# Another order of the seven half-size products in q, z and layer A's output projection

## The chip, the cores and the metric

The kernel runs on one core of a Trainium2 chip. The metric is the device time of one execution in microseconds, the median of several runs. The kernel before the change takes 2928.23 us (three runs, 2926.15 to 2930.01 us).

A core has five engines that run side by side, each with a queue that it works through in order: TensorE (PE in the profile, with PEld for the loading of its stationary operand), VectorE (DVE), ScalarE (ACT), GpSimd (POOL) and SyncE (SP), which here issues all transfers between the chip's main memory and the on-chip buffer. PE's results land in PSUM, a small memory that DVE and ACT read.

## The reference, cut to what matters

The model has one gated MLP layer (layer A), shared keys and values, and one layer of dilated attention (layer B), on 2048 tokens of width 1024, all in float32:

```python
def gmlp_layer(x, c, ...):                       # layer A
    h = rms_norm(x, norm_g) * (1 + scale) + shift
    u, v, z = jnp.split(h @ w_in, 3, axis=-1)
    ...
    y = u * mixed.reshape(bsz, s, A_WIDTH) * jax.nn.silu(z)
    return x + gate * (y @ w_out)                # dense_o: (2048 x 2048) @ (2048 x 1024)

def dilated_layer(x, c, kv_groups, ...):         # layer B
    h = rms_norm(x, norm_g) * (1 + scale) + shift
    qz = h @ w_in                                # dense_s: three q blocks and z, 1024 x 1024 each
    q = qz[..., :N_Q_HEADS * HEAD_DIM].reshape(bsz, s, N_Q_HEADS, HEAD_DIM)
    z = qz[..., N_Q_HEADS * HEAD_DIM:]
    q = rms_norm(q, q_norm_g) * (HEAD_DIM ** -0.5)
    for g, (window, d) in enumerate(DILATED_GROUPS):
        ...                                      # attention of group g; g = 2 is the widest
    y = o.reshape(bsz, s, B_WIDTH) * jax.nn.silu(z)
    return x + gate * (y @ w_out)
```

## The kernel before, in words

The tokens are worked in four quarters (Q = 0 to 3) of 512 tokens, four tiles of 128 rows each. A quarter goes through layer A (v, then u, then z, then the output projection), the norms of layer B, and `proj_B`: the third k/v block, the second, the q block of group 2, the first k/v block, the q blocks of groups 1 and 0, and z.

Float32 products are made of three matmuls each (`mm3`, line 278): every operand is split into a high and a low part (`split`, line 249: ACT writes the high part, DVE the rest), and high x high, low x high and high x low are added up in PSUM. One matmul takes a 128 x 128 stationary operand and 512 columns. Weights come by SP's transfers and, except for presplit ones, are split after they land (L251 on ACT, L252 on DVE).

**Seven half-size products.** q, z of layer B and, in quarters 1 to 3, layer A's output are multiplied as 2 x 2 blocks with seven products in place of eight. With A the tokens' operand and B the weights, s1 to s4 are sums of A's quadrants and t1 to t4 sums of B's, made ahead of time. The seven are 11·11, 12·21, s1·t1, s2·t2, s3·t3, s4·22 and 22·t4. Four results come out of them: rows 0 and 1 (tiles t = 0, 1) and rows 2 and 3 (t = 2, 3), each for column half n = 0 and n = 1:

- rows 0, 1, n = 0: 11·11 + 12·21
- U2 = 11·11 + s2·t2, a sum that the other three results share; U3 = U2 + s3·t3
- rows 2, 3, n = 1: U3 + s1·t1
- rows 2, 3, n = 0: U3 + 22·t4
- rows 0, 1, n = 1: U2 + s1·t1 + s4·22

`dense_s` (line 545) does this for a q block or z: 16 calls, four a quarter. It has two pairs of PSUM tiles, x and y, one tile for each row tile i; a product is 24 matmuls into one pair, and successive products alternate between the pairs. The flag `first` says whether a product starts its pair afresh or adds to what stands there. The order before is 11, s2, 12, s3, s1, 22·t4, s4·22; shared sums are kept in on-chip "sum tiles" (`sum_tile`, a pool of eight), to which DVE adds each further product out of PSUM (`add`, L575, ten additions of 128 x 512 a call); ACT copies the first one (L580, two a call). `evac` takes a finished result: for q (`q_block`, L1215) ACT squares, DVE and POOL make the row norms, and the tile goes to memory in `qd` by a store that is put off by some products (`stores`, `store_late`, L270); where a q result stands in PSUM itself, ACT copies it to a sum tile first (L1219). For z (`z_block`, L1235) ACT applies Silu (L1239) and the result goes to `zd`; in quarter 3 six of its eight tiles are held until later.

`dense_o` (line 456) does the same for layer A's output, with products of 48 matmuls, in two halves h, from weights that were combined and split before (`wtd`). Here `rows` names the halves in which all matmuls of row tile 0 go ahead of those of row tile 1. Copies are L503, additions L499, and the evacuation `ev` (L1134) adds a kept sum if it is given one (L1137), multiplies by the gate (L1138), adds the residual (L1109) and has ACT square the sum (L1110); after a row's second half, the row's norm is made and the normed row `xn` written (L1125). The hook, given as `(6, ...)`, puts `norm_T2` (L720) of rows 0 and 1 into the sixth product: 16 transposes on PE (L730), and on DVE the affine maps (L734) and low parts (L737). The same for rows 2 and 3 comes inside the k/v block that follows.

**What sets the order.** The program is written in the order of its Python calls, and work of other stages is mixed in as fillers: generators of which `tick` runs some steps after every few matmuls. In quarters 1 to 3 local attention fills layer A. In quarter 3 the attention of group 2 (`wide_attention`, L1170) fills the first k/v block and the q blocks of groups 1 and 0; it first flushes q2's stores, then loads, unit by unit, 128 rows of `qd` (L1319), taken at a stride of 16 rows from all quarters: column half n = 0 for a block's first unit, n = 1 for its second. A scheduler then orders each engine's instructions at compile time, by priority in the program's order and by when operands will be ready; all waits are put in by it. So one engine's order can differ from the written one, but on the chip it is fixed.

Of the kernel before, what the change touches and what calls it, by code (L numbers as in the profile page):

```python
# [34 lines left out]
def trunk(ctx, tc, out, x, c, a_ada_w, a_ada_b, a_norm_g, a_w_in, a_sgu_g, a_w_spatial,  # L35
# [420 lines left out]
    def dense_o(Q, ops, fs, evac, hook, after):  # L456
# [40 lines left out]
        def add(o, p, q):  # L497
            for i in range(2):
                nc.vector.tensor_tensor(o[i][:, 0:512], p[i], q[i][:, 0:512], ALU.add)  # L499

        def copy(pts, t):
            for i in range(2):
                nc.scalar.activation(t[i][:, 0:512], pts[i], AF.Copy)  # L503
            return t

        product(x, "11", "11", True, lambda: weights("21", 0), rows=(1,))
        u = copy(x, [sum_tile(f"ou{Q}{i}") for i in range(2)])
        operand("s4", "12")
        product(x, "12", "21", False, lambda: weights("22", 0), rows=(0, 1))
        for i in range(2):  # L510
            evac(i, 0, x[i], None)
        operand("s2", "11")
        product(y, "s4", "22", True, lambda: weights("t2", 0))
        q = copy(y, [sum_tile(f"oq{Q}{i}") for i in range(2)])
        operand("s1", "21")
# [3 lines left out]
        product(x, "s2", "t2", True, lambda: weights("t1", 0))  # L519
        add(u, x, u)  # L520
        operand("22", "22")
        product(y, "s1", "t1", True, lambda: weights("t3", 0), rows=(1,))
        w = [rp.tile([P, 512], F32, tag="raw", name=f"ow{Q}{i}") for i in range(2)]
        add(w, y, u)
        for i in range(2):
            evac(i, 1, w[i], q[i][:, 0:512])
        product(x, "s3", "t3", True, lambda: weights("t4", 0), hook)
        for i in range(2):
            evac(2 + i, 1, x[i], w[i])
        add(u, x, u)  # L530
        product(y, "22", "t4", True, after, rows=(1,))
        for i in range(2):
            evac(2 + i, 0, y[i], u[i][:, 0:512])
# [11 lines left out]
    def dense_s(ops, b, nm, evac):  # L545
# [24 lines left out]
        def tmp(n):  # L570
            return [sum_tile(f"{nm}{n}{i}") for i in range(2)]

        def add(o, p, q):
            for i in range(2):
                nc.vector.tensor_tensor(o[i][:, 0:512], p[i], q[i][:, 0:512], ALU.add)  # L575

        product(x, "11", "11", True)
        u2 = tmp("u")
        for i in range(2):
            nc.scalar.activation(u2[i][:, 0:512], x[i], AF.Copy)  # L580
        product(y, "s2", "t2", True)
        add(u2, y, u2)
        product(x, "12", "21", False)
        for i in range(2):
            evac(i, x[i], 0)
# [1127 lines left out]
```

## Time and profile before

| | us |
|---|---|
| runs: median (lowest to highest) | 2928.23 (2926.15 to 2930.01) |
| the profiled execution, first to last instruction | 2930.7 |
| PE busy | 2890.4 |
| DVE busy | 2166.7 |
| ACT busy | 1639.0 |
| POOL busy | 758.4 |

The profiled execution's own time is known by its span, 2930.7 us; it lies 2.5 us above the median of the runs. In the profile, a group's row gives line, engine, operation, output<-inputs, shapes and count, then the busy time in us, the mean of one in ns, and the engine's idle time before it with what ended it. In the windows view, each row is a stretch of the span in us from its start, with its length and the busy time of each engine (instructions in brackets), PE's granted clock, the DMA engines' busy share and GB/s. In the timeline view, each row has the start, the time until the last of the merged instructions ended, engine, line, operation, tensors and count, and in brackets idle time before and what released it. Neighbouring matmuls overlap in these rows: one takes about 390 ns but the next starts some 230 ns later (48 of them take 11.04 us). Names such as `pd_o3a` and `pd_o3b` are the PSUM pairs of dense_o in quarter 3, `pd_q31a` those of the q block of group 1 in quarter 3, `st_...` sum tiles.

### The profile page before, as it was taken

The page shows a single profiled execution, that of the slowest core. Times are in us where ns is not written, and L with a number is a line of the kernel's source. Part 1 is how long each engine was busy: PE and PEld are TensorE (multiplying, and loading weights), DVE is VectorE, ACT ScalarE, POOL GpSimd, SP SyncE. Part 2 cuts the span into 40 slices and gives each one's busy share as a digit, 9 for nine tenths or more (in the row PEclk, how much of TensorE's full clock was granted, in tenths as well). Part 3 has the DMA queues.
Part 4 walks back from the last instruction along what each step waited for, and adds up shares of the span by engine and source line. Part 5 has one row for each costly group of instructions (what it writes and reads, how often), then busy time and mean ns, then how long its engine had stood idle before and what let it go on. Part 6 is the DMA issues. An engine that isn't in the chain of part 4 may idle for free.

```text
span 2930.7 us, 45684 instructions
## 1 busy us (share of the span) xinstructions
PE 2890.4 (99%) x14642; PEld 2422.7 (83%) x14642; DVE 2166.7 (74%) x4038; ACT 1639.0 (56%) x3378; POOL 758.4 (26%) x1043
## 2 busy tenths in 40 slices
PE   8999999999999999999999999999999999999999
PEld 5788888888888878888888888888888888888887
DVE  6878666787777886877677776877769776888682
ACT  4323355767676365676555365674646366876441
POOL 1057522330000513501223213501414221122312
PEclk9999999999999999999999999999999999999999
DMA  8899976796889976887435976875337967789653
GB/s 285 272 311 336 308 244 184 257 306 203 282 294 315 334 241 210 265 289 249 158 120 202 344 226 203 296 262 162 105 109 260 322 202 224 256 271 332 216 172 112
DMA packets 393813, 713.54 MB, mean 243 GB/s; under 512 B 41723, under 2 KB 141277, under 8 KB 393573
## 3 DMA queue, kind: packets, MB, share of 16 engines
q1 hardware_dynamic: 393572, 710.63, 72.6%
q8 instruction: 116, 1.90, 0.3%
q14 instruction: 125, 1.02, 0.1%
HBM read 552.53 MB, written 157.95 MB: 242 GB/s over the span
## 4 chain that ended last, share of the span: by engine, by line
PE 40%; DMA 3%; issue 3%; DVE 3%; POOL 1%; ACT 1%; SPq 0%; POOLq 0%; ACTq 0%; DVEq 0%
PE po L1453 3%; PE pd_kv L280 3%; PE pd_z L324 2%; PE pd_z L322 2%; PE pd_z L323 2%; PE pd_o3a L280 1%; PE pd_u L322 1%; PE pd_u L324 1%; PE pd_u L323 1%; PE pd_o2a L280 1%; PE pd_v3b L280 1%; PE pf L1637 1%; PE pf L1638 1%; PE pf L1639 1%; DMA qt<-qd 1%
## 5 line engine op out<-in xcount | busy, mean ns | idle before, releaser
L280 PE MATMUL pd_kv<-w_kv,hkh 128*128 128x512 f32 x672 | 209.5, 393 | 1.4 <-DVE w_kv L252 1.3
L322 PE MATMUL pd_u<-hAh,w_u 128*128 128x512 f32 x512 | 207.5, 405 | 0.0
L322 PE MATMUL pd_z<-hAh,w_z 128*128 128x512 f32 x512 | 204.1, 399 | 0.0
L324 PE MATMUL pd_u<-hAh,w_u 128*128 128x512 f32 x512 | 201.0, 393 | 2.3 <-DVE w_u L252 2.3
L323 PE MATMUL pd_u<-hAl,w_u 128*128 128x512 f32 x512 | 200.2, 391 | 0.0
L324 PE MATMUL pd_z<-hAh,w_z 128*128 128x512 f32 x512 | 200.2, 391 | 0.0
L323 PE MATMUL pd_z<-hAl,w_z 128*128 128x512 f32 x512 | 199.5, 390 | 0.0
L1453 PEld LDWEIGHTS po<-kv,pT 128*128 128x128 f32 x1200 | 147.9, 192 | 13.0 <-ACT pT L1299 3.7
L251 ACT ACTIVATE w_u<-raw_u 128x512 fp32r<-128x512 f32 x128 | 79.2, 630 | 135.4 <-DMA raw_u<-in_a_w_in_dram 56.7
L1453 PE MATMUL po<-kv,pT 128*128 128x128 f32 x1200 | 151.2, 276 | 3.6 <-ACT pT L1299 2.5
L251 ACT ACTIVATE w_z<-raw_z 128x512 fp32r<-128x512 f32 x128 | 79.6, 628 | 133.9 <-PE pd_z L324 60.6
L280 PEld LDWEIGHTS pd_kv<-w_kv,hkh 128*128 128x128 f32 x672 | 125.9, 189 | 28.6 <-DVE w_kv L252 2.6
L1401 POOL TENSOR_TENSOR dg<-pr,ident 128x256 f32<-128x256 f32 x38 | 30.9, 813 | 437.2 <-DVE stat L1448 226.6
L252 DVE TENSOR_TENSOR w_z<-raw_z,w_z 128x512 fp32r<-128x512 f32 x128 | 109.4, 868 | 44.9 <-ACT w_z L251 44.6
L280 PE MATMUL pd_kv<-w_kv,hkl 128*128 128x512 f32 x336 | 131.2, 391 | 0.0
L1393 ACT ACTIVATE pr<-pr,stat,rt 128x256 f32<-128x256 f32 (+1 forms) x192 | 104.2, 544 | 33.2 <-DVE stat L1387 20.0
L1226 POOL TENSOR_SCALAR s_q<-s_q 128x4 f32<-128x4 f32 x96 | 26.6, 277 | 351.3 <-DVE s_q L1225 238.8
L252 DVE TENSOR_TENSOR w_u<-raw_u,w_u 128x512 fp32r<-128x512 f32 x128 | 94.1, 745 | 30.8 <-ACT w_u L251 30.0
L324 PEld LDWEIGHTS pd_u<-hAh,w_u 128*128 128x128 f32 x512 | 96.4, 188 | 24.2 <-DVE w_u L252 3.1
L251 ACT ACTIVATE w_q<-raw_q 128x512 fp32r<-128x512 f32 x144 | 88.8, 627 | 48.3 <-PE pd_kv L280 11.2
L252 DVE TENSOR_TENSOR w_q<-raw_q,w_q 128x512 fp32r<-128x512 f32 x144 | 95.8, 687 | 24.9 <-ACT w_q L251 22.9
L324 PEld LDWEIGHTS pd_z<-hAh,w_z 128*128 128x128 f32 x512 | 96.1, 188 | 20.7
(904 smaller groups left out, 8553.1 us busy)
## 6 DMA issues: line engine op xcount, KB each, us to landing
raw_q<-in_b_w_in_dram SPq DMA_DIRECT2D x144, 256.0 KB, 3.4
w_o<-wtd SPq DMA_DIRECT2D x72, 512.0 KB, 5.2
raw_u<-in_a_w_in_dram SPq DMA_DIRECT2D x128, 256.0 KB, 4.2
raw_z<-in_a_w_in_dram SPq DMA_DIRECT2D x128, 256.0 KB, 3.6
wtd<-cs SPq DMA_DIRECT2D x56, 512.0 KB, 4.1
qt<-qd SPq DMA_DIRECT2D x96, 260.0 KB, 3.6
raw_v<-in_a_w_in_dram SPq DMA_DIRECT2D x96, 256.0 KB, 4.1
od<-ot SPq DMA_DIRECT2D x96, 256.0 KB, 3.0
```

What stands on the lines that cost most here:

```text
L251: nc.scalar.activation(hi, src, AF.Copy)
L252: nc.vector.tensor_tensor(lo, src, hi.bitcast(F32), ALU.subtract)
L280: last_mm[0] = nc.tensor.matmul(pt, a, u[:, w, :], start=f, stop=e, skip_group_check=more)
L322: nc.tensor.matmul(pts[i], wh, hh[:, k, :], start=k == 0, stop=False)
L323: nc.tensor.matmul(pts[i], wh, hl[:, k, :], start=False, stop=False)
L324: nc.tensor.matmul(pts[i], wl, hh[:, k, :], start=False, stop=k == KT - 1)
L1393: nc.scalar.activation(pr[:, i, :], pr[:, i, :], AF.Exp, bias=mneg[:, i:i + 1], scale=u["rt"][:, h:h + 1], accum_out=lsum[:, i:i + 1])
L1401: nc.gpsimd.tensor_tensor(dg, prev, ident.unsqueeze(1).broadcast_to([P, hp, P]), ALU.mult)
L1453: nc.tensor.matmul(po[:, h * P:(h + 1) * P], u["pT"][h // hp][:, h % hp, j, :], u["kv"][:, j, kh, 1, :], start=j == 0, stop=j == nk - 1)
L1637: nc.tensor.matmul(pt, yb[:, 0, k, :], w_[:, 0, :], start=k == 0, stop=False)
L1638: nc.tensor.matmul(pt, yb[:, 0, k, :], w_[:, 1, :], start=False, stop=False)
L1639: nc.tensor.matmul(pt, yb[:, 1, k, :], w_[:, 0, :], start=False, stop=k == KT - 1)
```

## The change

In `dense_o` and `dense_s` the seven products get the order 11, 12·21, s2, s1, then s3 and s4·22 (dense_s) or s4·22 and s3 (dense_o), then 22·t4. The pair that holds 11·11 is copied by ACT, goes on to take s2·t2 (so it holds U2) and is copied again, then takes s3·t3 (U3) and at last 22·t4, so that rows 2, 3 with n = 0 stand in PSUM as a whole. The other pair takes 12·21, and then s1·t1, which ACT copies, and s4·22 on top. Each of the other three results is one PSUM pair plus one copied sum, added by DVE. The additions of `dense_s` fall from ten to six a call and its copies rise from two to six; in `dense_o` the additions fall from twelve to six (those in `ev` included) and the copies rise from four to six. The operand splits of `dense_o` move with their products, and `rows` is set for other products. In `q_block` the copy out of PSUM moves from rows 0, 1 to rows 2, 3 (n = 0), and in `z_block` the tiles that are not held in quarter 3 change likewise, and their stores are issued at once.

```diff
--- before.py
+++ after.py
@@ -494,43 +494,37 @@
             for h in range(2):
                 split(ops[n][:, h, 0], ops[n][:, h, 1], fs[h][src])
 
-        def add(o, p, q):
+        def copy(pts, nm):
+            t = [sum_tile(f"{nm}{Q}{i}")[:, 0:512] for i in range(2)]
             for i in range(2):
-                nc.vector.tensor_tensor(o[i][:, 0:512], p[i], q[i][:, 0:512], ALU.add)
-
-        def copy(pts, t):
-            for i in range(2):
-                nc.scalar.activation(t[i][:, 0:512], pts[i], AF.Copy)
+                nc.scalar.activation(t[i], pts[i], AF.Copy)
             return t
 
         product(x, "11", "11", True, lambda: weights("21", 0), rows=(1,))
-        u = copy(x, [sum_tile(f"ou{Q}{i}") for i in range(2)])
+        p1 = copy(x, "op")
+        operand("s2", "11")
+        product(y, "12", "21", True, lambda: weights("t2", 0), rows=(1,))
+        for i in range(2):
+            evac(i, 0, y[i], p1[i])
+        operand("s1", "21")
+        product(x, "s2", "t2", False, lambda: weights("t1", 0))
+        u2 = copy(x, "ou")
         operand("s4", "12")
-        product(x, "12", "21", False, lambda: weights("22", 0), rows=(0, 1))
-        for i in range(2):
-            evac(i, 0, x[i], None)
-        operand("s2", "11")
-        product(y, "s4", "22", True, lambda: weights("t2", 0))
-        q = copy(y, [sum_tile(f"oq{Q}{i}") for i in range(2)])
-        operand("s1", "21")
+        product(y, "s1", "t1", True, lambda: weights("22", 0), rows=(1,))
+        p5 = copy(y, "oq")
         for f in fs:
             nc.vector.tensor_tensor(f["11"], f["22"], f["11"], ALU.subtract)
         operand("s3", "11")
-        product(x, "s2", "t2", True, lambda: weights("t1", 0))
-        add(u, x, u)
+        product(y, "s4", "22", False, lambda: weights("t3", 0), rows=(0, 1))
+        for i in range(2):
+            evac(i, 1, y[i], u2[i])
         operand("22", "22")
-        product(y, "s1", "t1", True, lambda: weights("t3", 0), rows=(1,))
-        w = [rp.tile([P, 512], F32, tag="raw", name=f"ow{Q}{i}") for i in range(2)]
-        add(w, y, u)
+        product(x, "s3", "t3", False, lambda: weights("t4", 0), hook, rows=(1,))
         for i in range(2):
-            evac(i, 1, w[i], q[i][:, 0:512])
-        product(x, "s3", "t3", True, lambda: weights("t4", 0), hook)
+            evac(2 + i, 1, x[i], p5[i])
+        product(x, "22", "t4", False, after, rows=(0, 1))
         for i in range(2):
-            evac(2 + i, 1, x[i], w[i])
-        add(u, x, u)
-        product(y, "22", "t4", True, after, rows=(1,))
-        for i in range(2):
-            evac(2 + i, 0, y[i], u[i][:, 0:512])
+            evac(2 + i, 0, x[i], None)
         return nxt.pop()
 
     def load_wo(n, q):
@@ -567,38 +561,32 @@
                 with tc.issue_after(last_ld[0].ins):
                     job()
 
-        def tmp(n):
-            return [sum_tile(f"{nm}{n}{i}") for i in range(2)]
-
-        def add(o, p, q):
+        def copy(pts, n):
+            t = [sum_tile(f"{nm}{n}{i}") for i in range(2)]
             for i in range(2):
-                nc.vector.tensor_tensor(o[i][:, 0:512], p[i], q[i][:, 0:512], ALU.add)
+                nc.scalar.activation(t[i][:, 0:512], pts[i], AF.Copy)
+            return t
+
+        def add(o, p, r, n):
+            for i in range(2):
+                nc.vector.tensor_tensor(o[i][:, 0:512], p[i], o[i][:, 0:512], ALU.add)
+                evac(i + r, o[i], n)
 
         product(x, "11", "11", True)
-        u2 = tmp("u")
+        p1 = copy(x, "u")
+        product(y, "12", "21", True)
+        add(p1, y, 0, 0)
+        product(x, "s2", "t2", False)
+        u2 = copy(x, "v")
+        product(y, "s1", "t1", True)
+        p5 = copy(y, "w")
+        product(x, "s3", "t3", False)
+        add(p5, x, 2, 1)
+        product(y, "s4", "22", False)
+        add(u2, y, 0, 1)
+        product(x, "22", "t4", False)
         for i in range(2):
-            nc.scalar.activation(u2[i][:, 0:512], x[i], AF.Copy)
-        product(y, "s2", "t2", True)
-        add(u2, y, u2)
-        product(x, "12", "21", False)
-        for i in range(2):
-            evac(i, x[i], 0)
-        product(y, "s3", "t3", True)
-        u3 = tmp("v")
-        add(u3, y, u2)
-        product(x, "s1", "t1", True)
-        add(u3, x, u3)
-        for i in range(2):
-            evac(i + 2, u3[i], 1)
-        product(y, "22", "t4", False)
-        c21 = tmp("w")
-        add(c21, y, u2)
-        for i in range(2):
-            evac(i + 2, c21[i], 0)
-        product(x, "s4", "22", False)
-        add(u2, x, u2)
-        for i in range(2):
-            evac(i, u2[i], 1)
+            evac(i + 2, x[i], 0)
 
     def dense_s2(ops, bs, nm, evac, late):
 
@@ -1214,7 +1202,7 @@
 
         def q_block(g):
             def ev(t, src, n):
-                if t < 2 and n == 0:
+                if t >= 2 and n == 0:
                     c_ = sum_tile(f"qc{g}{Q}{t}")
                     nc.scalar.activation(c_[:, 0:512], src, AF.Copy)
                     src = c_
@@ -1234,12 +1222,12 @@
 
         def z_block(_):
             def ev(t, src, n):
-                held = Q == NQ - 1 and (t, n) not in ((0, 0), (1, 0))
+                held = Q == NQ - 1 and (t, n) not in ((2, 0), (3, 0))
                 zt = src[:, 0:512] if held else evt(f"zb{n}{Q}_{t}")
                 nc.scalar.activation(zt, src[:, 0:512], AF.Silu)
                 put = lambda: nc.sync.dma_start(zd[rows(t), n * 512:(n + 1) * 512], zt)
-                if Q == NQ - 1:
-                    stores.append([-100 if held else 3, put])
+                if held:
+                    stores.append([-100, put])
                 else:
                     put()
             dense_s(hb, 3, f"z{Q}b", ev)
```

## The prediction

> **What bounds the kernel now.** I read the page's busy shares first, then the busy time by windows cut at the stages that the change touches, then who waited for whom on PE, then the order of time around two joints.
>
> ```profile
> span 2930.7 us, 45684 instructions
> ...
> PE 2890.4 (99%) x14642; PEld 2422.7 (83%) x14642; DVE 2166.7 (74%) x4038; ACT 1639.0 (56%) x3378; POOL 758.4 (26%) x1043
> ```
>
> PE (TensorE) is busy for 2890.4 of 2930.7 us; DVE (VectorE) and ACT (ScalarE) have slack over the whole span. The span is 2.5 us above the median of the runs, 2928.23; differences are worked out in the span and applied to the median. A change of under 0.2% (5.9 us) is about what a measurement of this kernel can't tell from none.
>
> ```profile
> core 0: us, PE busy (x) PEld busy (x) DVE busy (x) ACT busy (x) POOL busy (x), PEclk, DMA share, GB/s
> 520.00:638.00 118.00, 118.00 (x537) 97.63 (x536) 91.44 (x148) 79.82 (x144) 50.58 (x79) 1.00 0.83 278
> 930.00:1090.00 160.00, 156.63 (x825) 131.18 (x823) 134.40 (x289) 85.06 (x190) 44.30 (x60) 1.00 0.83 292
> 1579.00:1732.00 153.00, 151.13 (x786) 126.91 (x785) 126.95 (x260) 74.59 (x158) 41.16 (x59) 1.00 0.86 298
> 1791.00:1909.00 118.00, 118.00 (x538) 97.59 (x537) 91.93 (x147) 79.11 (x143) 53.99 (x79) 1.00 0.82 272
> 2226.00:2376.00 150.00, 147.99 (x767) 124.70 (x766) 120.79 (x249) 76.33 (x159) 38.28 (x54) 1.00 0.83 286
> 2414.00:2450.00 36.00, 32.69 (x166) 26.92 (x165) 17.80 (x44) 16.59 (x42) 7.63 (x18) 0.95 0.62 195
> 2450.00:2614.00 164.00, 159.69 (x1069) 142.86 (x1069) 132.82 (x336) 135.23 (x382) 26.21 (x55) 1.00 0.79 253
> 2614.00:2656.00 42.00, 41.21 (x185) 33.21 (x184) 28.49 (x53) 25.01 (x48) 9.00 (x15) 1.00 0.98 359
> ```
>
> The rows from 520 and 1791 hold two q blocks and z of quarters 0 and 2: PE has no idle time at all there. The three rows of 150 to 160 us hold layer A's output (dense_o) and the first k/v block of quarters 1 to 3: 3.37, 1.87 and 2.01 us idle. The last three are in quarter 3: the k/v block in which the wide attention starts (3.31 idle), the two q blocks with attention between their products (4.31), and z (0.79). Idle time within the change's reach is thus 15.7 us, 0.5% of the span. No engine's total says more than that.
>
> **The change, part by part.** Removed and added work has these prices:
>
> ```profile
> L499 DVE TENSOR_TENSOR st_ou<-pd_o2a,st_ou 128x512 f32<-128x512 f32 x4 | 2.6, 682 | 0.0
> ...
> L575 DVE TENSOR_TENSOR st_q11v<-pd_q11a,st_q11u 128x512 f32<-128x512 f32 x2 | 1.4, 688 | 1.8 <-PE pd_q11a L280 1.8
> ...
> L580 ACT ACTIVATE st_q31u<-pd_q31b 128x512 f32<-128x512 f32 x2 | 1.1, 584 | 0.0
> ```
>
> Each of the 16 dense_s calls goes from 10 DVE additions to 6 and from 2 copies to 6; each of the 3 dense_o calls from 12 additions to 6 and from 4 copies to 6. That is 64 + 18 = 82 additions less, 82 x 0.685 = 56 us of DVE, and 64 + 6 = 70 copies more, 70 x 0.584 = 41 us of ACT. The matmuls, their weights' loads and the stores stay the same in number.
>
> dense_s in quarters 0 to 2 and q2 of quarter 3: nothing. PE is saturated, and successive products still alternate between the two PSUM pairs, so each read has a whole product's time to finish, as now. If that cover failed, a product would wait for one 0.58 or 0.69 us read at most; 0 is taken. A q call fills all eight sum tiles before and after. The copies after products 3 and 4 now take tiles that the previous call's stores must have left; were one late, ACT would stand, with the weights' splits queued behind the copy, and PE after them. Today the q evacuation's copy after product 3 takes its tile at that same place in windows without idle time, so this too is 0.
>
> dense_o: two joints become tight, since a product now adds to the pair that the product just before it filled. From product 5 on (y, after s1·t1) the wait is for an ACT copy. That joint exists today after product 1, with the products' rows sorted as here:
>
> ```profile
> 1595.27 0.60 ACT L503 ACTIVATE st_ou<-pd_o2a 128x512 f32<-128x512 f32 x1 [0.48 <-PE pd_o2a L280]
> ...
> 1596.51 2.91 PE L280 MATMUL pd_o2a<-w_o,yo 128*128 128x512 f32 x12
> ```
>
> The copy ends at 1595.87 and PE shows no idle time: 0 for this one. The other is from product 6 (x, s3·t3) to 7 (x, 22·t4): PE must wait until DVE has read x in the evacuation, and the hook puts norm_T2's DVE work right there. Today product 7 goes to y and nobody waits:
>
> ```profile
> 2298.13 0.69 DVE L499 TENSOR_TENSOR ow<-pd_o3b,st_ou 128x512 f32<-128x512 f32 x1 [6.00 <-PE pd_o3b L280]
> 2299.92 1.12 DVE L1459 SCALAR_TENSOR_TENSOR ot<-st_o,stat,po 128x128 f32<-128x128 f32 x4 [1.09 <-PE po L1453]
> ...
> 2314.95 0.99 DVE L734 TENSOR_SCALAR h_b_0k<-pt_b,affk,affk 128x256 f32<-128x256 f32 x2 [2.09 <-PE pt_b L730]
> ...
> 2320.63 1.28 DVE L1137 TENSOR_TENSOR xo<-pd_o3a,ow 128x512 f32<-128x512 f32 x2
> ...
> 2325.05 1.28 DVE L499 TENSOR_TENSOR st_ou<-pd_o3a,st_ou 128x512 f32<-128x512 f32 x2
> ...
> 2329.26 0.68 DVE L252 TENSOR_TENSOR w_kv<-raw_kv,w_kv 128x512 fp32r<-128x512 f32 x1
> ```
> ```profile
> 2317.44 11.04 PE L280 MATMUL pd_o3b<-w_o3t,yo 128*128 128x512 f32 x48
> ...
> 2329.99 0.50 PE L280 MATMUL pd_kv<-w_kv,hkh 128*128 128x512 f32 x1 [1.06 <-DVE w_kv L252]
> ```
>
> Product 7 starts at 2317.44, and x is read from 2320.63 on. Product 6 gets sorted rows, so x0 is complete 12 matmuls before x1, and six of them come before the hook. I take x0's read to run before the hook's DVE work, in the 2.09 us for which DVE stood idle ahead of 2314.95: the first two rows show that order today, an addition of product 5's first half ahead of an attention step (L1459) that the program writes earlier. Then only x1's read is late. PE comes to x1 after 12 of 48 matmuls, at 2317.44 + 2.76 = 2320.20; the read takes x0's old place and ends at 2320.63 + 0.68 = 2321.31: 1.1 us of wait. Quarters 2 and 1 by the same sum:
>
> ```profile
> 1673.39 0.97 PE L280 MATMUL pd_o2b<-w_o2t,yo 128*128 128x512 f32 x3 [0.58 <-DMA w_o2t<-wtd]
> ...
> 1675.82 1.28 DVE L1137 TENSOR_TENSOR xo<-pd_o2a,ow 128x512 f32<-128x512 f32 x2
> ...
> 1026.30 1.07 PE L280 MATMUL pd_o1b<-w_o1t,yo 128*128 128x512 f32 x4
> ...
> 1029.44 1.28 DVE L1137 TENSOR_TENSOR xo<-pd_o1a,ow 128x512 f32<-128x512 f32 x2
> ```
>
> 1675.82 + 0.68 - (1673.39 + 2.76) = 0.35 us, and 1029.44 + 0.68 - (1026.30 + 2.76) = 1.06, for which I take 0.5, as an attention step may stand between. Joint 6 to 7: +2.0; bounds 0 (all reads early) and +10.8 (rival 1).
>
> The k/v block after it gains. PE waits there for weights that DVE splits behind dense_o's last additions:
>
> ```profile
> PE pt_b L730 <- DVE xn L1125: 2.4, 5, 0.5
> PE pd_kv L280 <- DVE w_kv L252: 1.3, 2, 1.1
> ...
> PE pd_kv L280 <- DVE w_kv_0b L252: 1.0, 1, 1.0
> ```
>
> Ahead of the split at 2329.26 the pair of additions at 2325.05 goes, and one of the last product's (0.68): 1.9 us, more than the longest of these waits, 1.1. So the 2.3 us of w_kv and w_kv_0b go: -2.3, bounds 0 and -2.3. Next late are the 2.4 us for xn. They follow a chain over ACT and POOL that stays, so I leave them; if they went too, another -2.4.
>
> Quarter 3's k/v block is where the reordering moves an event. Half n = 0 of q2, which the wide attention's first unit loads, is now finished by the last product instead of the sixth. On SP's queue today:
>
> ```profile
> 2420.89 0.33 SPq L1319 DMA_DIRECT2D qt<-qd  x1
> ...
> 2421.79 1.93 SPq L1232 DMA_DIRECT2D qd<-st_q32u  x2
> 2427.83 0.32 SPq L1319 DMA_DIRECT2D qt<-qd  x1
> ```
> ```profile
> 2430.52 0.17 DVE L1339 COPY rt<-qt 128x8 f32<-128x8 f32 x1 [5.49 <-DMA qt<-qd]
> ...
> 2435.89 1.12 DVE L1383 SCALAR_TENSOR_TENSOR pr<-dist,rt,ps 128x128 f32<-128x128 f32 x4
> ```
> ```profile
> 2426.95 0.60 PE L1343 MATMUL pq<-ident,qt 128*128 128x128 f32 x4
> ...
> 2437.11 0.63 PE L1343 MATMUL pq<-ident,qt 128*128 128x128 f32 x4 [1.59 <-DVE pr L1383]
> ...
> 2442.15 1.16 PE L1374 MATMUL ps<-kT,qT 128*128 128x128 f32 x8 [1.28 <-ACT qT L1346]
> ```
>
> The chain to the last store keeps its length but for two additions of 0.69 us, for which two copies of 0.58 us on ACT come. The first load (2420.89) goes out before that store (2421.79); the second waits for it until 2427.83 and is used at 2430.52. Afterwards the first waits too, and behind it on SP stand the weights' loads of q1. Unit 0's transposes at 2426.95 would stand 3.6 us. But unit 0's next DVE step runs only at 2435.89, behind k/v work that keeps its place, and the waits of 1.59 and 1.28 at 2437 and 2442 are then used up by the earlier one. Net +0.5; bounds -2.9 (both waits gone) and +5.8 (rival 2). In the q blocks from 2450 to 2614 DVE is at 81% and ACT at 82%: 8 additions go (5.5 us) and 8 copies come (4.7 us) on engines equally full: 0, bounds -4.3 (all their idle time) and +4.7 (the copies all on the path). z of quarter 3: 0. Its last two stores now go out at once and hold up SP's loads for the final stage by at most two ACT passes over the last product, 2 x 0.58 = 1.2 us; on the other side stand its 0.8 us of idle time.
>
> Sum: +2.0 - 2.3 + 0.5 = +0.2, so 2928.4 us.
>
> **Rivals.** 1, slower: x0's read stays behind the hook's DVE work. Then product 7 starts after 2321.31, 1676.50 and 1030.12: waits of 3.9, 3.1 and 3.8, +10.8, less the 2.3 of the k/v block, +8.5: 2936.7. It decides where x0's addition stands after the first L734. For it: the hook's work is written earlier; against: the row at 2298.13.
>
> 2, slower: the attention's late start isn't absorbed, because the clock drops after the wait:
>
> ```profile
> 2439.00:2447.00 8.00, 6.27 (x27) 4.83 (x27) 5.32 (x15) 6.91 (x22) 0.00 (x0) 0.79 0.66 218
> ```
>
> Today's waits there end in a granted clock of 0.79 over 8 us, 1.7 us lost. A wait of 3.6, a second such drop and the 0.5 give +5.8: 2934.2. The Trainium skill, "TensorE: Matmul & The Clock Gate", Part 1, says that an idle window of about 3.4 us halves the clock until PE has been busy for about as long; this row agrees that the drop follows idle time, though no single wait here was that long. By that rule alone rival 1's waits of 3.8 and 3.9 would cost more as well.
>
> 3, faster: the waits in quarter 3 hang on DVE's queue more than on ACT's and end with the additions; of 15.7 us idle some 7 go: 2921. For it: the release by DVE at 2437.11; against: ACT is as full.
>
> **How the numbers follow.** Forecast 0.53 (within 4 us), rival 3 0.25, rivals 1 and 2 0.11 each. Rival 2's price lies at the bound, so half of it counts as slower: faster 0.25, same 0.58, slower 0.17. The range reaches 3 us below rival 3 and just over rival 1: 2918 to 2938, with some 0.1 left out on either side.
>
> **What would show it.** PE idle before product 7 of dense_o under 1.5 us a quarter, with x0's addition ahead of the first L734; no wait on w_kv; q windows of quarters 0 to 2 still without idle time; the wide attention's first load behind all stores of q2, and an idle time in 2414 to 2450 near 3.8 us. Wrong if PE waits over 3 us before product 7, or if ACT becomes the releaser of most waits from 2450 to 2614.

## The result, and the profile after

| | before | after |
|---|---|---|
| runs: median (lowest to highest) | 2927.19 (2921.05 to 2930.01) | 2940.27 (2938.78 to 2944.14) |
| ratio, 95% interval | | 1.0052 (1.0040 to 1.0064) |
| profiled execution: span | 2930.7 | 2938.6 |

The change makes the kernel 0.5% slower, some 13 to 15 us. The two profiles differ by only 7.9 us: in 23 to 35 further runs on the chips of the experiments the kernel before had medians of 2924.3 to 2925.5, so its profiled execution was one of its longer ones. Below, sizes come from the ratios, places from the profiles.

The page of the kernel after, its span and busy shares:

```profile
span 2938.6 us, 45628 instructions
...
PE 2891.4 (98%) x14642; PEld 2428.7 (83%) x14642; DVE 2120.4 (72%) x3956; ACT 1673.1 (57%) x3448; POOL 750.6 (26%) x1043
```

The counts are as forecast: 82 instructions less on DVE, 70 more on ACT. DVE is busy for 46 us less, and the span is longer. The windows of the stages that the prediction showed, set to where those stages now lie, and last the start of the final phase:

```profile
core 0: us, PE busy (x) PEld busy (x) DVE busy (x) ACT busy (x) POOL busy (x), PEclk, DMA share, GB/s
520.00:638.00 118.00, 118.00 (x537) 97.62 (x537) 87.10 (x138) 85.30 (x155) 47.82 (x79) 1.00 0.83 278
928.00:1089.00 161.00, 156.48 (x826) 131.59 (x825) 130.72 (x283) 86.68 (x192) 42.03 (x60) 1.00 0.83 291
1579.00:1736.00 157.00, 151.88 (x785) 128.10 (x784) 125.06 (x253) 76.31 (x159) 41.81 (x59) 0.99 0.80 280
1796.00:1914.00 118.00, 118.00 (x537) 97.61 (x536) 85.34 (x137) 87.27 (x156) 49.23 (x79) 1.00 0.84 279
2228.00:2385.00 157.00, 150.56 (x771) 126.96 (x770) 119.76 (x244) 79.00 (x162) 37.03 (x54) 0.99 0.77 264
2423.00:2455.00 32.00, 30.31 (x171) 25.78 (x169) 16.92 (x43) 18.21 (x47) 6.87 (x15) 1.00 0.64 201
2455.00:2617.00 162.00, 159.58 (x1065) 142.75 (x1064) 128.64 (x329) 136.59 (x384) 25.93 (x56) 1.00 0.79 256
...
2653.00:2665.00 12.00, 7.92 (x36) 6.50 (x35) 4.64 (x13) 6.53 (x18) 0.00 (x0) 0.86 0.96 347
```

The q and z blocks of quarters 0 and 2 still leave PE no idle time; in quarter 1 they leave 0.4 us. dense_o with its k/v block goes from 3.37, 1.87 and 2.01 us idle to 4.52, 5.12 and 6.44. Quarter 3's k/v block falls from 3.31 to 1.69, the two q blocks behind it from 4.31 to 2.42. The wait that is left in the k/v block wasn't there before:

```profile
2447.96 1.13 PE L1362 MATMUL ps<-kT,qT 128*128 128x128 f32 x8 [1.69 <-DVE stat L1375]
```

New are 4.08 us of idle time, at a clock of 0.86, at the start of the final phase. PE's waits name both places:

```profile
PE pf L1625 <- ACT yb L1588: 4.1, 1, 4.1
...
PE pd_o3a L280 <- ACT hob L737: 3.8, 1, 3.8
PE pd_o2a L280 <- ACT hob L737: 3.8, 1, 3.8
PE pt_b L718 <- DVE xn L1113: 3.6, 4, 1.0
...
PE pyb L1586 <- DVE pT L1285: 2.0, 1, 2.0
...
PE pd_o1a L280 <- DVE xo L1125: 1.2, 1, 1.2
```

`pd_o2a` and `pd_o3a` are the pair x ahead of product 7. (Lines from layer A on are 12 lower than before: L722, L725 and L1125 were L734, L737 and L1137.) The profile names ACT as the releaser in two of the three, but no matmul on x needs `hob`. The timeline of DVE, and under it PE's, in quarter 3 show who it was:

```profile
2316.57 1.11 DVE L1447 SCALAR_TENSOR_TENSOR ot<-st_o,stat,po 128x128 f32<-128x128 f32 x4
2319.00 1.00 DVE L722 TENSOR_SCALAR h_b_0k<-pt_b,affk,affk 128x256 f32<-128x256 f32 x2 [1.31 <-PE pt_b L718]
...
2324.22 0.54 DVE L722 TENSOR_SCALAR h_b_6k<-pt_b,affk,affk 128x256 f32<-128x256 f32 x1
2324.67 1.28 DVE L1125 TENSOR_TENSOR xo<-pd_o3a,st_oq 128x512 f32<-128x512 f32 x2
```
```profile
2315.50 3.02 PE L280 MATMUL pd_o3a<-w_o3t,yo3s 128*128 128x512 f32 x12
...
2320.02 1.62 PE L280 MATMUL pd_o3a<-w_o3t,yo3s 128*128 128x512 f32 x6
2325.46 7.76 PE L280 MATMUL pd_o3a<-w_o3t,yo 128*128 128x512 f32 x26 [3.82 <-ACT hob L737]
```

x0's last six matmuls are the first half of the row at 2315.50, so x0 could be read from about 2317. DVE stood idle for 1.31 us until 2319.00, then worked through the hook, and read x0 at 2324.67; PE began product 7 at 2325.46, just after that 0.69 us read ended. In the windows behind the wait the clock falls:

```profile
2321.00:2325.00 4.00, 0.64 (x3) 0.19 (x1) 3.85 (x8) 4.00 (x10) 0.00 (x0) 1.00 1.02 411
2325.00:2329.00 4.00, 3.54 (x10) 2.84 (x11) 3.88 (x7) 3.38 (x8) 0.00 (x0) 0.68 0.86 347
```

To compare stages I use one more quantity, the lost time: over a stage's matmuls, the time from each start to the next start, less the median of that for the same line and shape. It holds waits and slow clock alike.

| lost, us | before | after |
|---|---|---|
| dense_o, quarters 1, 2, 3 | 3.8, 2.3, 1.1 | 5.6, 7.2, 8.5 |
| the k/v block after it | 3.2, 1.9, 2.8 | 2.0, 1.2, 1.3 |
| quarter 3: k/v block, last two q blocks | 6.3, 7.1 | 2.3, 5.2 |
| quarter 3: z, final phase | 1.8, 6.2 | 4.2, 9.0 |

By these rows, in order: +14.1, -3.4, -5.9 and +5.3. All other stages together are some 2 us shorter, mostly by single waits that come and go between executions (v of quarters 1 and 3, 1.9 and 1.8).

### The profile page after: what moved, and what is told of

Its sections match the earlier page's. It is cut to its first block, busy times and chain, and to the rows that moved or that the text cites. A ratio compares the mean times of both kernels' runs of the same rounds, so it can differ in the third digit from the quotient of the medians.

```text
span 2938.6 us, 45628 instructions
## 1 busy us (share of the span) xinstructions
PE 2891.4 (98%) x14642; PEld 2428.7 (83%) x14642; DVE 2120.4 (72%) x3956; ACT 1673.1 (57%) x3448; POOL 750.6 (26%) x1043
## 4 chain that ended last, share of the span: by engine, by line
PE 83%; DVE 5%; DMA 4%; issue 3%; POOL 2%; ACT 2%; SPq 0%; POOLq 0%; DVEq 0%; ACTq 0%
PE pd_kv L280 8%; PE pd_z L324 4%; PE pd_z L322 4%; PE pd_z L323 4%; PE po L1441 4%; PE pd_u L322 4%; PE pd_u L324 4%; PE pd_u L323 4%; PE pd_o L280 3%; PE pm L1029 2%; PE pd_o3a L280 1%; PE pd_o2a L280 1%; PE pd_v1b L280 1%; PE pd_v3b L280 1%; PE pd_v3a L280 1%
## 5 line engine op out<-in xcount | busy, mean ns | idle before, releaser
L1389 POOL TENSOR_TENSOR dg<-pr,ident 128x256 f32<-128x256 f32 x38 | 31.5, 830 | 438.0 <-DMA w_o<-wtd 226.8
```

The costliest lines, as they stand in the source:

```text
L1389: nc.gpsimd.tensor_tensor(dg, prev, ident.unsqueeze(1).broadcast_to([P, hp, P]), ALU.mult)
```

## The experiments

Ratios are against runs of the kernel before on the same chip, with 95% intervals; 0.001 is 2.9 us. First: which part of the change costs, and is it the order of the read?

**dense_o alone, and everything else alone.** The first kernel is the one before with the diff's hunk in `dense_o`, the second the changed one without it.

```diff
         product(x, "11", "11", True, lambda: weights("21", 0), rows=(1,))
-        u = copy(x, [sum_tile(f"ou{Q}{i}") for i in range(2)])
+        p1 = copy(x, "op")
...
```

> The kernel before with the changed dense_o alone; q, z and layer A's v stay as they were. Theory (x0 is read behind the hook's DVE work, and each wait of over 3 us ahead of product 7 is followed by a stretch at half clock): waits of some 4.0 us in Q2 and in Q3 and of 1 to 2 us in Q1 ahead of the transposes of product 7, half clock behind the two long ones (1.6 us each), less 2 to 3.5 us of the key/value blocks' waits: +8 to +11 us against the kernel before. Rival 1 (the loss is made in q and z: the ACT evacuations and the late key loads at the start of the final phase): this kernel is within 3 us of the kernel before.

> The changed kernel with the old dense_o; only q, z and v1 to v3 are reordered. Theory (dense_o carries the loss): +1 to +4 us against the kernel before: 4 us of wait and a stretch at half clock (1 us) between z of Q3 and the final phase, against some 3 us that end in Q3's k/v block and second q block. Rival 1 (the loss is made in q and z): +8 to +13 us. Where it comes out below the kernel before, the reordering of q and z is a gain by itself and dense_o costs more than the whole difference.

Measured: 1.0035 (1.0022 to 1.0048), +10.2 us, with waits of 1.2, 3.8 and 3.8 us ahead of product 7, for which the profile names DVE's `xo` in quarter 2 as well; and 1.0008 (0.9997 to 1.0019), +2.3 us, with 4.5 us at the start of the final phase. dense_o carries most of the loss.

**Another pool for the read's target.** `evt` tiles come from one pool of six; the hook's four `h_b` tiles and the tiles `xo`, into which x is read, are all from it.

```diff
-                tmp = evt(f"xo{Q}_{n}_{t}")
+                tmp = (rp.tile([P, 512], F32, tag="raw", name=f"xo{Q}_{n}_{t}") if t >= 2 and n else
+                       evt(f"xo{Q}_{n}_{t}"))
```

> The changed kernel, with the tiles into which tokens 256 to 511 of the second half of dense_o's output are scaled taken from another pool, so that they needn't wait for a slot behind the hook's four tiles; nothing else differs. Theory: the read of the first tile of x0 (and most of the second) goes ahead of the hook's DVE work, the waits ahead of product 7 fall from 1.2/3.8/3.8 us to under 1.5 us in each quarter, the half clock behind them goes, and the time falls by 8 to 12 us against the changed kernel, to about the kernel before (2926 to 2932). Rival 2 (ACT, loaded with 14 further copies in each dense_o, is what is late: the profile lists ACT's operand as the releaser of the wait in Q3): the waits stay at 3 us or more and the time within 3 us of the changed kernel.

DVE's timeline of this kernel in quarter 3 (L1126 is the read):

```profile
2321.41 0.69 DVE L1126 TENSOR_TENSOR xo<-pd_o3a,st_oq 128x512 f32<-128x512 f32 x1
...
2323.47 0.99 DVE L722 TENSOR_SCALAR h_b_0k<-pt_b,affk,affk 128x256 f32<-128x256 f32 x2
...
2329.14 0.68 DVE L1126 TENSOR_TENSOR xo<-pd_o3a,st_oq 128x512 f32<-128x512 f32 x1
```

x0's read now stands ahead of the hook's first step in all three quarters, as I had assumed; x1, complete only after the transposes, is still read behind all but the last of its steps. The waits were 1.9 us in quarter 3, 1.6 in quarter 2 and none of note in quarter 1; the ratio 1.0034 (1.0021 to 1.0047), some 5 us better than the change and not the 8 to 12 expected. (A dense_o call has two copies more than before, not 14.) So the pool decides where x0's read stands. That its slots are handed out in the program's order is how I read this.

**The hook in product 7, later, and earlier.** The hook's place is a number of units of six matmuls, 1.4 us each: 6 in the changed kernel, which runs it behind product 6's seventh unit. In the first kernel it runs behind product 7's first unit, not ahead of it.

```diff
-        product(x, "s3", "t3", False, lambda: weights("t4", 0), hook, rows=(1,))
+        product(x, "s3", "t3", False, lambda: weights("t4", 0), rows=(1,))
...
-        product(x, "22", "t4", False, after, rows=(0, 1))
+        product(x, "22", "t4", False, after, hook, rows=(0, 1))
...
-            ahead_kv = dense_o(Q, yo, fs, ev, (6, lambda: (operands(), first())),
+            ahead_kv = dense_o(Q, yo, fs, ev, (0, lambda: (operands(), first())),
```

> The changed kernel with the hook (transposes, affine and splits for the k/v block of the first 256 tokens) called ahead of product 7's first unit in place of product 6's seventh: both reads of x0 then stand ahead of the hook's DVE work. Theory: waits ahead of product 7 fall to the joint of before (0.5 to 1.5 us), no half clock there, but the hook's operands come some 5 us later than in the changed kernel, with ten units left in which to be made; dense_o gains 8 to 12 us, the k/v block may give back 0 to 4: 2927 to 2934. Rival 2 (ACT is late): no gain, within 3 us of the changed kernel.

```diff
-            ahead_kv = dense_o(Q, yo, fs, ev, (6, lambda: (operands(), first())),
+            ahead_kv = dense_o(Q, yo, fs, ev, (7, lambda: (operands(), first())),
```

> The changed kernel with the hook called one unit (1.4 us) later, behind product 6's last unit. Theory: the waits ahead of product 7 grow by 1.4 us, to 5.2 to 5.5 us in Q2 and Q3 and to 2.5 to 4 us in Q1, where half clock now follows as well: 4 to 7 us slower than the changed kernel, 18 to 23 us above the kernel before. Rival (something that ends at a fixed time): the waits stay at 4.0 us and the time within 2 us of the changed kernel.

The third has 4 in place of the 6.

> The changed kernel with the hook called two units (12 matmuls, 2.7 us) earlier, at product 6's fifth unit in place of its seventh: the reads of x0 stay behind the hook's DVE work, which begins 2.7 us earlier. Theory: the waits ahead of product 7 fall by the same 2.7 us, from 4.0 to 1.2 to 1.4 us in Q2 and Q3 and to nothing in Q1, and no half clock follows them; 8 to 11 us faster than the changed kernel, to 3 to 7 us above the kernel before. Rival (the wait ahead of product 7 is made by something that ends at a fixed time, a load or ACT's copies): waits as in the changed kernel, time within 3 us of it.

Measured: 1.0018 (1.0009 to 1.0026), 1.0062 (1.0044 to 1.0079) and 1.0045 (1.0031 to 1.0059). With the hook in product 7 the waits for `xo` fall to 0.5 us and less, and 10 us come back; but in quarter 2 product 7 then waits 2.1 us for its weights' load. The later and the earlier hook, PE's waits of each:

```profile
PE pd_o2a L280 <- ACT hob L737: 5.2, 1, 5.2
PE pd_o3a L280 <- ACT hob L737: 5.2, 1, 5.2
...
PE pd_o1a L280 <- DVE xo L1125: 1.5, 1, 1.5
```
```profile
PE pd_o1a L280 <- DVE xo L1125: 2.5, 1, 2.5
...
PE pd_o3a L280 <- DVE xo L1125: 1.8, 1, 1.8
...
PE pd_o2a L280 <- DVE xo L1125: 1.1, 1, 1.1
```

In quarter 2 the wait follows the hook, 1.1, 3.8 and 5.2 us for the fifth, seventh and eighth unit: 2.7 us for two units and 1.4 for one. Nothing that ends at a fixed time does that. The later hook costs 18 us against the kernel before, 3 more than the change and not the 4 to 7 expected, since in quarter 1 the wait was 1.5 us and not 2.5 to 4. The earlier hook missed in the other quarters and in its sum. In quarter 3 its transposes waited 1.6 us for `xn`, which moved the hook less than two units. In quarter 1 the wait grew: attention matmuls (`po`) that keep PE at work ahead of product 7 in the changed kernel stand behind the wait here, and the read came at the same time, 1027.86 against 1027.85. dense_o loses 16.6 us there against 21.3, yet the time is only some 2 us better. What takes the rest isn't settled; that profile has a wait of 2.2 us, with half clock behind it, between quarter 1's z and the v that follows.

**Product 7 on the other accumulator.** Nobody then waits for the reads of x:

```diff
+        u3 = copy(x, "op")
         for i in range(2):
             evac(2 + i, 1, x[i], p5[i])
-        product(x, "22", "t4", False, after, rows=(0, 1))
+        product(y, "22", "t4", True, after, rows=(0, 1))
         for i in range(2):
-            evac(2 + i, 0, x[i], None)
+            evac(2 + i, 0, y[i], u3[i])
```

> The changed kernel, with dense_o's product 7 on the other accumulator (y, whose last addition is long done) in place of x: x is copied by ACT behind product 6 and the copy is added to y at the end, as in the kernel before. Two copies more on ACT, two instructions more on VectorE, and product 7 waits for no read of x. Theory (the read of x0 behind the hook's DVE work is the loss): no wait ahead of product 7 in any quarter, no half clock there; the time falls by 9 to 13 us against the changed kernel, to 0 to 4 us above the kernel before. Rival (the hook is hit as such, by ACT's or DVE's load in this stretch): the waits reappear at the transposes or at the k/v block's first load, and the gain is under 5 us.

> The kernel before with the changed dense_o whose product 7 goes to the other accumulator; q, z and v1 to v3 are the old ones. It tells what of the remaining 5 us above the kernel before, in the run with product 7 on y, is dense_o's and what is q's and z's. Theory (dense_o costs nothing but the wait ahead of product 7; the rest is q's order, which puts the final phase's attention units in another order): within 2.5 us of the kernel before, final phase's lost time 5 to 6 us. Rival (dense_o's other moves cost as well): 4 to 6 us above it.

Measured: 1.0018 (1.0009 to 1.0027), 10 us better than the change; and, with this dense_o alone, 1.0005 (0.9995 to 1.0014). PE's timeline of the first, quarter 3, has no wait between product 6 and 7, and PE's waits of the second show that those for the k/v block's weights are back with the two additions:

```profile
2313.43 1.62 PE L280 MATMUL pd_o3a<-w_o3t,yo3s 128*128 128x512 f32 x6
2314.89 8.32 PE L280 MATMUL pd_o3b<-w_o3t,yo 128*128 128x512 f32 x36
```
```profile
PE pd_kv L280 <- DVE w_kv L252: 1.2, 2, 1.0
...
PE pd_kv L280 <- DVE w_kv_0b L252: 1.0, 1, 1.0
```

The wait ahead of product 7 and what follows it are thus worth 9 to 10 us, and what else moves in dense_o costs nothing that shows.

**q and z apart.** In these kernels both forms of `dense_s` and of its callers' `ev` stand side by side.

```diff
+    def dense_sz(ops, b, nm, evac):
...
-            dense_s(hb, 3, f"z{Q}b", ev)
+            dense_sz(hb, 3, f"z{Q}b", ev)
```

> The kernel before with the reordered products for q alone; z and dense_o are the old ones. Theory (z's order puts SP and ACT late at the start of the final phase, q's order costs nothing and lets the wide attention in Q3 start with fewer waits): the first load of pf waits for nothing, Q3's k/v block and second q block lose 3 to 6 us less than in the profiled run of before; 0 to 5 us faster than the kernel before. Rival (q's own copies cost what the run with q and z together shows): 1 to 5 us slower.

> The kernel before with the reordered products for z alone. Theory: the wait ahead of the first matmul of the final phase of 4.0 to 5.0 us in Q3, half clock behind it (1.1 to 1.7 us); nothing in Q0 to Q2; +3 to +7 us against the kernel before. Rival: within 2 us of the kernel before, and the cost seen with q and z together comes from q.

> As the run with product 7 on y, and with the old order for z: what is left of the change is q's order and dense_o's order with its last product as in the kernel before. Theory: no wait ahead of product 7, none ahead of the final phase; 3 to 7 us under the run with product 7 on y alone, that is from 5 us faster to 1 us slower than the kernel before. Rival (the instructions removed from VectorE, not the waits, set the time): equal to the run with product 7 on y.

Measured: 1.0013 (1.0004 to 1.0022), 1.0013 (1.0001 to 1.0025) and 1.0022 (1.0012 to 1.0032). For z alone the wait at the start of the final phase is 1.9 us, not 4 to 5. It is 1.9 us too in the kernel with product 7 on y, in which q and z are both new, so its length isn't a matter of these two alone. For q my theory falls: it costs some 4 us, and the old z doesn't give anything back to the kernel with product 7 on y.

**What z does.** ACT's timeline of the changed kernel at the start of the final phase:

```profile
2654.56 0.60 ACT L1227 ACTIVATE zb<-pd_z3bb 128x512 f32<-128x512 f32 x1 [3.40 <-PE pd_z3bb L280]
2659.06 0.40 ACT L1554 ACTIVATE og<-og,stat 128x128 f32<-128x128 f32 x1 [3.91 <-DMA og<-od]
2659.37 0.58 ACT L1227 ACTIVATE zb<-pd_z3bb 128x512 f32<-128x512 f32 x1
2659.85 1.07 ACT L1588 ACTIVATE yb<-pyb 128x512 fp32r<-128x512 f32 x2
```

One scaling of `og` stands 3.91 us on its load; behind it queue the second Silu and the copy `yb`, for which PE waits. The load went out late, as SP's queue shows:

```profile
2635.43 9.01 SPq L259 DMA_DIRECT2D raw_z3bt<-wt  x4
...
2648.42 2.19 SPq L1540 DMA_DIRECT2D og<-od  x3
```

SP spent 9.0 us on four loads of z's last weights and issued `og` 31.5 us after z's first matmul, in the kernel before 28.8. The load then took 10.6 and 10.0 us to land. In the two kernels whose wait is 1.9 us it went out after 28.8 and 29.0 us, and over the kernels with z's new order and this scaling in place, 28.8 to 32.2 us go with waits of 1.9 to 4.7: the later SP comes to the load, the longer PE waits. (In the kernel before the scaling stands ahead of `yb` as well, from 2653.53, and PE waits 0.2 us.) What holds SP up longer isn't settled. The edit puts the scaling behind the copies, in the kernel with q and z reordered and the old dense_o:

```diff
...
-            make_yb(0)
-        ys[1] = prepare(1, ogs[1])
+            act = make_yb(0)
+        with tc.issue_after(act.ins):
+            ys[1] = prepare(1, ogs[1])
```

> The run with the reordered q and z and the old dense_o, with one edit at the start of the final phase: the scaling of the second tile's attention output on ACT, which waits for its load, is put behind the copies of the first tile's transposed output in ACT's order. Theory: the wait of 4.6 us ahead of the first matmul of the final phase is ACT standing on that load with the copy behind it; it falls to under 1 us, the half clock behind it goes, and the time falls by 4 to 6 us against the same kernel without the edit, to 1 to 4 us under the kernel before. Rival (the copy waits for the last products of z in any case, or the load is needed right after): the wait reappears within the next 10 us and the gain is under 1.5 us.

```profile
2641.97 1.28 ACT L1233 ACTIVATE zb<-pd_z3bb 128x512 f32<-128x512 f32 x2 [3.40 <-PE pd_z3bb L280]
2643.15 1.08 ACT L1594 ACTIVATE yb<-pyb 128x512 fp32r<-128x512 f32 x2
2645.77 2.46 ACT L1560 ACTIVATE og<-og,stat 128x128 f32<-128x128 f32 x8 [1.53 <-DMA og<-od]
```

Silu and copies run at once, the scaling waits alone, and PE's wait is gone (z's lost time 0.2 for 4.6 us). Measured 0.9998 (0.9989 to 1.0007): about 3 us better than without the edit, not the 4 to 6 expected, and level with the kernel before.

**What q does.** Six profiles with the old order in quarter 3's last two q blocks (the kernel before and those below included) lose 5.2 to 6.2 us in the final phase, twelve with the new order 6.2 to 12.0, median 9.0. Two kernels split q there:

```diff
         def q_block(g):
+            old = Q == NQ - 1 and g < 2
...
-            dense_s(hb, g, f"q{Q}{g}", ev)
+            (dense_sz if old else dense_s)(hb, g, f"q{Q}{g}", ev)
```

The second has `not (...)` around the condition. Two more put both mends on the whole change, and the last of these also keeps the old order in those two blocks.

> The kernel before with the reordered products for q alone, and of these without Q3's last two q blocks (the second and the first, after the k/v block), which keep the old order: ten of the twelve q blocks are reordered. Theory (q's cost sits in Q3's last two q blocks, which set in which order the final phase's attention units come): the final phase loses 5 to 6.2 us as with the old order; within 2.5 us of the kernel before. Rival (q's copies cost in every quarter): the same time as with all q reordered, 2 to 5 us above the kernel before, and a final phase that loses 8 to 10 us isn't needed for it.

> The kernel before with only Q3's last two q blocks in the new order. Theory: the final phase loses 8 to 9.7 us, as in every profile with all q reordered, against 5.2 to 6.2 us with the old order; 1 to 5 us slower than the kernel before, less what these two blocks and the k/v block ahead of them gain (0 to 3 us). Rival: the final phase loses 5 to 6.2 us and the time is within 2 us of the kernel before.

> The whole change with both mends: product 7 on the other accumulator, and the scaling of the second tile behind the copies of the first at the start of the final phase. Theory: the two mends add, since their waits lie in different stages: 2 to 5 us below the run with product 7 on y alone (1.0018), that is 0 to 4 us above the kernel before. Rival: no better than that run.

> The whole change with both mends and the old order in Q3's last two q blocks. Theory: no wait ahead of product 7, none ahead of the final phase, and a final phase that loses 5 to 6.2 us: from 4 us under to 1 us above the kernel before. Rival (the waits ended return elsewhere, since PE is at 98% and the instructions removed from VectorE were not what it waited for): within 2 us of the kernel before on either side.

Measured: 1.0005 (0.9996 to 1.0014), 1.0014 (1.0005 to 1.0023), 1.0013 (1.0003 to 1.0023) and 1.0007 (0.9998 to 1.0016), with 5.2, 12.0, 11.2 and 5.8 us lost in the final phase. The first two intervals overlap, but with the final phase they point one way: the two blocks carry q's cost, through a stage that they don't belong to. The two mends together gain 1.5 us over product 7 on y alone, not 2 to 5, where the wait for `yb` had been 1.9 us; and the last kernel missed its theory, 4 us under to 1 us above. DVE's timeline in the final phase, of the kernel with only these two blocks new, and of the last one:

```profile
2723.37 2.18 DVE L1622 SCALAR_TENSOR_TENSOR og<-og,wst,og 128x128 f32<-128x128 f32 x8
2726.24 1.92 DVE L1392 COPY rt<-qt 128x8 f32<-128x8 f32 x1 [0.68 <-DMA qt<-qd]
2728.07 0.68 DVE L1350 COPY pT<-pp 128x512 f32<-128x512 f32 x1
```
```profile
2725.07 0.64 DVE L1617 SCALAR_TENSOR_TENSOR og<-og,wst,og 128x128 f32<-128x128 f32 x2 [1.84 <-ACT og L1614]
2725.64 0.68 DVE L1345 COPY pT<-pp 128x512 f32<-128x512 f32 x1
2726.58 0.17 DVE L1387 COPY rt<-qt 128x8 f32<-128x8 f32 x1 [0.26 <-DMA qt<-qd]
```

PE's transposes `pyb` wait for the copy `pT`. In the first kernel it stands behind a small copy that waits for a load of `qt` and then takes 1.92 us, and PE waits 2.3 us; in the second it stands ahead of it, and PE waits 0.7. All twelve profiles have the small copy ahead, at 1.9 to 2.0 us, and lose 1.4 to 2.5 us at this place; all six have it behind, at 0.17 us, and lose 0.8 to 0.9. Why the copy takes so long there, and which moved instruction made the scheduler turn the two around, isn't settled. It is a part of q's cost: the first kernel also loses 1.3 us at a slow clock behind this wait, and 4 us at and behind an earlier one of 2.3 us that I can't explain. With all three losses mended the change comes out at +2 us, between -0.6 and +4.7: no version beats the kernel before.

## Why the prediction was wrong

- **Joint 6 to 7 (+2.0): the step that failed.** "I take x0's read to run before the hook's DVE work" did not hold. The row that I leaned on, the addition at 2298.13, wrote a tile of another pool (`ow`, from `rp`); x0's read writes `xo`, from the pool of the hook's own tiles, and changing that pool alone put it ahead, in each of the three quarters. An order seen for one instruction said nothing of another whose target comes from elsewhere. The idle 2.09 us that I meant for the read were there again, 1.31 of them, and stayed idle. Of quarter 3's 7.4 us, 1.7 are a wait for a weights' load that dense_o alone doesn't show.
- **Rival 1 was the case**, at a chance of 0.11. Its waits of 3.9, 3.1 and 3.8 us (quarters 3, 2, 1) came as 3.8, 3.8 and 1.2; that the sums, 10.8 and 8.8, lie near each other is in part luck, as quarters 1 and 2 missed in opposite directions. Its time, 2936.7, lacked the half clock behind two of them, 8 matmuls at 0.43 in place of 0.23 us, 1.6 us each, and the losses of q and z. The sentence on the Trainium skill's page "TensorE: Matmul & The Clock Gate", Part 1, had it: by that rule waits over 3.4 us cost more as well, and the trace agrees, 0.68 behind 3.8 us. I left it out of rival 1's sum.
- **The k/v block (-2.3):** right in kind. The waits for `w_kv` and `w_kv_0b` are gone, also with the hook in product 7, where quarter 3 has no long wait that could have given DVE the time; they return when two additions do. The waits for `xn` grew from 2.4 to 3.6 us.
- **Quarter 3's k/v block (+0.5):** it gained 4.0 us, beyond the bound of -2.9. The first load went out behind all stores of q2, as said, but the two waits of 1.59 and 1.28 us that I had called used up only in part both ended. One of 1.69 came later in the block, ahead of 2447.96, so the idle time fell by 1.6 us. Most of the rest is the slow clock behind the two waits, which rival 2 priced at 1.7 us and the bound left out: the block's granted clock went from 0.95 to 1.00. In all profiles the median lost there is 4.8 us with q2 in the old order (5) and 2.3 in the new (13).
- **The last two q blocks (0):** right for themselves, within the bounds: 4.31 to 2.42 us idle here, and over all profiles a median of 6.4 us lost there in either order. The sum had no term for what their order does to the final phase, +3 us; I looked for the effect only in the stage that was edited.
- **z of quarter 3 (0, at most +1.2):** 4.1 us and a slow stretch. I priced SP behind the last stores; what stood was ACT, behind a load that SP issued 2.7 us later, still ahead of z's last two stores.
- **q and z of quarters 0 to 2 (0):** right, 118.00 of 118.00 us busy in quarters 0 and 2, and 0.4 us idle in quarter 1.

Of the 15 us by the ratio, the joint makes 10. q alone and z alone cost some 4 us each, both together 2; the intervals don't allow a finer split. Rival 3 fell: DVE's 46 us less bought PE nothing where PE was already busy.

## What to carry to other kernels

When an accumulator is reused by the very next product, the reader's place in its engine's queue becomes a place on the critical path: find every instruction that the compiled order can put ahead of it, and check that its target tile doesn't come from the same pool as theirs. Where a scheduler orders the engines, an edit can turn two instructions around in a later stage, so compare that stage too. Work taken off an engine that PE didn't wait for was worth nothing here, while a joint that the change tightened cost at once.

## What the runs showed of the hardware

Half clock came after waits well under 3.4 us, and not in every execution. At 135 us PE waits for a split of `w_u`, a part of the kernel that no edit touches. In eleven of the profiled executions 2.0 us were lost there; the clock dropped behind it in nine. The two that follow stood idle for 1.88 us each. They are the kernel before, in which it dropped, and the one with the scaling behind the copies:

```profile
136.00:140.00 4.00, 2.12 (x12) 1.85 (x11) 4.00 (x7) 0.00 (x0) 0.00 (x0) 0.91 0.37 96
140.00:144.00 4.00, 4.00 (x14) 3.42 (x14) 3.93 (x8) 1.60 (x3) 0.00 (x0) 0.50 1.01 308
```
```profile
136.00:140.00 4.00, 2.52 (x15) 2.26 (x16) 4.00 (x8) 0.06 (x1) 0.00 (x0) 1.00 0.45 133
140.00:144.00 4.00, 4.00 (x28) 3.59 (x27) 3.93 (x8) 1.60 (x3) 0.00 (x0) 1.00 0.94 298
```

With the same wait before it, the second window holds 14 matmuls at a clock of 0.50 in one and 28 at 1.00 in the other. Over all 18 profiles, from layer A's first matmul on, at least three matmuls at about twice their time followed 1 of some 93 losses of 1.0 to 1.4 us, 4 of 46 of 1.4 to 1.9, 20 of 35 of 1.9 to 2.4, 4 of 10 of 2.4 to 3.5, and all 10 of more than that; how far behind the wait one counts changes these by one or two. The Trainium skill, "TensorE: Matmul & The Clock Gate", Part 1, gives about 3.4 us of idle time for the drop, in windows that run freely. A free-running window agrees with a drop that one execution shows and another doesn't, but waits of 2 us often sufficed here, so for the length the measurement decides. For a sum: behind those 10 another 1.6 to 2.7 us were lost, mostly 1.7, and an estimate for one of 2 us, dropping in 20 of 35, is about half of that on average.
